# FFN output with eight passing pairs: factors formed in three pieces, bank merges behind later splits, norm scale loaded mid-block

## The chip, the cores and the metric

The kernel runs on one core of one Trainium2 chip. A core has TensorE for matrix products, VectorE (DVE), ScalarE (ACT) and GpSimd (POOL) for elementwise work, SyncE (SP) which here only issues transfers, and 16 DMA engines that all queues share. Each engine works through its own instructions in program order; semaphores tie the engines together. The metric is the device time of one execution in microseconds.

## The reference, cut to what matters

The program is one layer of a decoder: 512 tokens of width 2048, a sparse attention mixer, a SwiGLU feed-forward part, and a final norm. The change touches only the last product of the feed-forward part, and the final norm behind it:

```python
def swiglu(h, w_in, w_out):
    z = h @ w_in
    a, b = z[..., :D_FF], z[..., D_FF:]
    return (jax.nn.silu(a) * b) @ w_out

h = h + swiglu(rmsnorm(h, ffn_norm_g[i]), ffn_w_in[i], ffn_w_out[i])
return rmsnorm(h, final_norm_g)
```

D_FF is 5632, so the last product is (512 x 5632) times (5632 x 2048), in float32.

## The kernel before

**Numbers in two parts.** Float32 accuracy is had from a faster format: each operand is split into a high part (ScalarE copies it into the rounded format) and a low part (VectorE subtracts the high part from the original). A product is three matmuls, high times high, low times high and high times low (`three`, L271 to 274). So each operand costs ScalarE one pass and VectorE one pass before TensorE can use it. Tiles named whi and wlo hold split weights, thi and tlo a split plain factor or split weight sums, ah and al the seven split factors of a pair.

**Units.** The inner dimension is cut into 22 pairs of 256 rows (j), the output columns into four blocks of 512 (b). A unit n is one pair in one block; `ORDER` gives the order of the pairs in each block, `seq` is the list of all 88 units, and the last four (`N_TAIL`) are done together at the end, token tile by token tile. A plain unit is 24 matmuls of 512 columns into the four banks `po`. A unit whose pair is in `SEVEN[b]` uses a Strassen-like scheme: seven products in place of eight, 42 matmuls of 256 columns, into `po` and four more banks `qs` (`seven_unit`). It needs four sums of the weight blocks (`weight_sums`, on VectorE: four 256-column operations, then a split of 768 columns into thi and tlo) and seven factors of the left side (`form`).

**Forms.** `form(j)` loads the pair's left side from DRAM tensor `d_a` into `scratch`, which is the last quarter of the accumulator `acc` before it is needed, makes four sums on VectorE, and splits seven pieces in three steps (256, 512 and 1024 columns; ScalarE L1198, VectorE L894). Five pairs (`KEPT`) stay in SBUF in the pool `asl`. The others are passing pairs: their ah and al go to DRAM (`d_s`, by POOL, L1202) and are loaded again for each later visit (L1222, `load_seven`, POOL) into the two buffers of the pool `ast`. There are nine passing pairs, added block by block: three in block 0, seven in block 1, nine in blocks 2 and 3.

**Order in an iteration.** The program is written in the order in which each engine works; nothing rearranges it. For unit n the loop does: `prepare(n + 1)`, the whole form of the next unit if it is one that forms; `W2.take`, the split of the weights of unit n + 1 (L93 on ScalarE, L95 on VectorE) and the loads of the raw weights behind it (SP, L77, three buffers); `split_a(n + 1)`, the split of a plain unit's left side (L1116), and the load of a later one into one of two homes, `tt` or `rawx` (SP, L1108); the matmuls of unit n; after the block's last seven `merge_sums`, one ScalarE copy and six VectorE additions that bring the four banks `qs` into `acc`; the reloads of passing pairs; and one step of `todo`. After a block, `add` brings `po` into `acc`, and `todo` becomes `ready(b)`, which loads 512 columns of the final norm's scale (`gf`, POOL, L1280) and then, token tile by token tile, sums the squares (ScalarE, L1284) and multiplies by the scale (VectorE, L1285).

**Residual.** What the earlier part left, `d_r`, is loaded into `acc` by POOL: three quarters at the start of this stage (L1226, 3 MB), the last quarter when the last form is done with `scratch` (L1182, 1 MB).

Buffers that matter for waits: whi and wlo four each, thi and tlo two each, `tt` and `rawx` one each, raw three, `ast` two pairs.

Of the kernel before, what the change touches and what calls it, by code (L numbers as in the profile page):

```python
# [10 lines left out]
F32 = mybir.dt.float32  # L11
F32R = mybir.dt.float32r
I32 = mybir.dt.int32
AF = mybir.ActivationFunctionType
# [19 lines left out]
ORDER = [tuple(range(22)),  # L34
# [3 lines left out]
TP_GAP, HN_GAP = 40, 48  # L38
RESYNC = 14
SPREAD = 2560  # L40
# [128 lines left out]
def nsa_block(ctx: ExitStack, tc: tile.TileContext, x, rel_bias, mix_g, ffn_g, fin_g, w_in, w_out,  # L169
              pos_k, w1k, w2k, pos_v, w1v, w2v, f_in, f_out, onehot, out):  # L170
    nc = tc.nc
    mm, act, dve, pool = nc.tensor.matmul, nc.scalar.activation, nc.vector, nc.gpsimd
# [163 lines left out]
    with ExitStack() as st1:  # L336
# [11 lines left out]
        with ExitStack() as st0:  # L348
# [6 lines left out]
            for t in range(NT):  # L355
# [11 lines left out]
            oh = xp.tile([NB + 1, UL + 16 * CL], F32, name="oh")  # L367
# [60 lines left out]
            p = ps1.tile([128, 2, 32], F32, name="tr")  # L428
# [3 lines left out]
            for c0, c1 in ((0, 512), (512, UL), (UL, UL + 496), (UL + 496, UL + 992)):  # L432
                p = ps1.tile([H, 512], F32, name="mlp" if c1 % 1024 == 512 or c1 == UL + 496 else "tr")
# [88 lines left out]
        for i in range(8):  # L522
# [10 lines left out]
            if i == 1:  # L533
                p = ps1.tile([128, 128], F32, name="tr")
# [27 lines left out]
        p = ps1.tile([96, G, 128], F32, name="tr")  # L562
# [8 lines left out]
    with ExitStack() as st2:  # L571
# [206 lines left out]
        for h in range(H):  # L778
# [11 lines left out]
            seq = [(b, kt) for kt in (3, 2, 1, 0) for b in (0, 1)] + [(-1, 0)]  # L790
# [23 lines left out]
    acc = accp.tile([128, NT, D], F32, name="acc")  # L814
# [75 lines left out]
    def f32(t):  # L890
        return t.bitcast(F32)

    def sub(o, a, b):
        dve.tensor_tensor(o, a, b, op=OP.subtract)  # L894

    def plus(o, a, b):
        dve.tensor_tensor(o, a, b, op=OP.add)
# [156 lines left out]
    with tc.tile_pool(name="tmp", bufs=1) as tmp:  # L1054
        todo = sums(tmp)
# [24 lines left out]
        for u in range(2):  # L1080
            k = slice(8 * u, 8 * u + 4)
# [7 lines left out]
    seq = [(b, j) for b in range(4) for j in ORDER[b]]  # L1089
# [20 lines left out]
    def split_a(n):  # L1110
# [36 lines left out]
    for n, (b, j) in enumerate(seq):  # L1147
        if j in SEVEN[b]:
            W2.sums[n] = weight_sums(n)
# [18 lines left out]
    acc = late.tile([128, NT, D], F32, name="acc")  # L1168
    late.tile([128, 16], F32, name="late_gap")
    asl = ctx.enter_context(tc.tile_pool(name="asl", bufs=len(KEPT)))  # L1170
    ast = ctx.enter_context(tc.tile_pool(name="ast", bufs=2))
    late2 = ctx.enter_context(tc.tile_pool(name="late2", bufs=1))
    ss = [late2.tile([128, 4], F32, name=f"sf{t}") for t in range(NT)]
    scratch = acc[:, :, 1536:]
    forms = [n for n, (b, j) in enumerate(seq) if j in SEVEN[b] and (not b or j not in SEVEN[b - 1])]
    visits = [n for n, (b, j) in enumerate(seq) if j in SEVEN[b] and j not in KEPT]

    def load_form(i):
        if i < len(forms):
            nc.sync.dma_start(scratch[:, :2], d_a[seq[forms[i]][1]].rearrange("p (n c) -> p n c", n=2))  # L1180
        else:
            pool.dma_start(scratch, d_r[:, :, 1536:].rearrange("t p c -> p t c"))  # L1182

    def form(j):

        a, m = scratch[:, :2], scratch[:, 2:]
        a11, a21, a12, a22 = a[:, 0, :256], a[:, 0, 256:], a[:, 1, :256], a[:, 1, 256:]
        s1, s3, s2, s4 = m[:, 0, :256], m[:, 0, 256:], m[:, 1, :256], m[:, 1, 256:]
        h, l = ((asl if j in KEPT else ast).tile([128, 1792], F32R, name=f"a{x}") for x in "hl")
        plus(s1, a21, a22)  # L1190
        sub(s3, a11, a21)
        sub(s2, s1, a11)
        sub(s4, a12, s2)
        for c0, c1, src in ((0, 256, a11), (256, 768, a[:, 1]), (768, 1792, m)):
            oh, ol = h[:, c0:c1], l[:, c0:c1]
            if c1 - c0 == 1024:
                oh, ol = (x.rearrange("p (n c) -> p n c", n=2) for x in (oh, ol))
            act(oh, src, AF.Copy)  # L1198
            sub(ol, src, f32(oh))
        if j not in KEPT:  # L1200
            for i, x in enumerate((h, l)):
                pool.dma_start(d_s[j, i], x.bitcast(F32))  # L1202
        keep_seven(j, h, l)
# [8 lines left out]
    n_visit = [0]  # L1212

    def load_seven(n):

# [13 lines left out]
    def prepare(n):  # L1229

        if n in forms:
            form(seq[n][1])
            load_form(forms.index(n) + 1)
            n_visit[0] += n in visits

    def plain_tile(n, w, t, first, last):
        for k in range(2):
# [20 lines left out]
    def merge_sums(b):  # L1258
# [8 lines left out]
        act(u3, qs["p1"], AF.Copy)  # L1267
# [8 lines left out]
    def ready(b):  # L1276

        c = slice(512 * b, 512 * (b + 1))
        gf = late2.tile([128, 512], F32, name="gf")
        pool.dma_start(gf, fin_g[None, c].to_broadcast([128, 512]))  # L1280
        yield
        for t in range(NT):
            junk = late2.tile([128, 1024], F32, name="m")[:, :512]
            act(junk, acc[:, t, c], AF.Square, accum_out=ss[t][:, b:b + 1])  # L1284
            dve.tensor_tensor(acc[:, t, c], acc[:, t, c], gf, op=OP.mult)  # L1285
            yield

    w8, todo = [], iter(())
    n, na = 0, 1
    for b in range(4):  # L1290
        units = ORDER[b][:-N_TAIL] if b == 3 else ORDER[b]
        po = [pf.tile([128, 512], F32, name=f"f{i}") for i in range(4)]
        qs = {x: pf.tile([128, 512], F32, name=f"f{i}") for i, x in enumerate(("p1", "p5", "p6", "p7"))}
        first7 = next(j for j in units if j in SEVEN[b])
        last7 = [j for j in units if j in SEVEN[b]][-1]
        started = False
        for i, j in enumerate(units):
            left = len(units) - 1 - i if b == 3 else 9
            prepare(n + 1)
            w = W2.take(max(1, 3 - left))  # L1300
            while na <= n + 1 + max(0, 2 - left):
                split_a(na)
                na += 1
            if j in SEVEN[b]:
                seven_unit(n, w, first7)
            else:
                for t in range(NT):
                    plain_tile(n, w, t, not started, b < 3 and i == len(units) - 1)
            started = True
            if j == last7:  # L1310
                merge_sums(b)
            load_seven(n)
            if i >= 2:
                next(todo, None)
            n += 1
        if b < 3:
            for t in range(NT):
                add(t, b, po[t])
            todo = ready(b)
    c = slice(1536, 2048)  # L1320
    gf = late2.tile([128, 512], F32, name="gf")
    pool.dma_start(gf, fin_g[None, c].to_broadcast([128, 512]))
    act(warm, epsc, AF.Sqrt)
    for t in range(NT):
        for i in range(N_TAIL):
# [10 lines left out]
        for cb in range(4):  # L1336
            c4 = slice(512 * cb, 512 * (cb + 1))
            src = acc[:, t, c4]
# [33 lines left out]
```

## Time and profile before

| what | value |
|---|---|
| median of 3 runs | 2225.47 us (2224.15 to 2227.64) |
| profiled execution | 2224.97 us |
| its span | 2223.1 us |
| TensorE matmul, busy | 2159.1 us, 97% |
| VectorE, busy | 1573.6 us, 71% |
| ScalarE, busy | 937.9 us, 42% |
| granted clock of TensorE, mean | 0.992 |

The span runs from the first to the last instruction of the profiled execution; what lies between it and that execution's time is start and end of the program. A row of a timeline gives the start from the span's beginning and the duration, both in us, then engine, line, operation, and output and input tiles, and in brackets the idle time before it with what ended it. A row of a group gives busy us and mean ns, and behind the second bar the engine's idle time just before. Matmuls overlap in the pipeline, so a unit is measured from its first matmul's start to the next unit's first start, not by busy time. Where a helper records the operation, all its uses have the same line (L894 is every subtraction of the helper `sub`, L897 every addition of `plus`), so that tiles must be read with it: al<-acc,ah is a form's low part, tlo<-tt,thi of 768 columns the split of weight sums.

### The profile page before, as it was taken

Reading aid. Unit: us, or ns where it says so; the run is one execution under the profiler, and the core shown is the slowest. Engines: PE = TensorE matmul, PEld = TensorE weight load, DVE = VectorE, ACT = ScalarE, POOL = GpSimd, SP = SyncE. Lnnn points to the kernel's source line nnn. Section 1 sums busy time; section 2 is a strip of 40 time slices with the busy share of each in tenths; the row PEclk is TensorE's granted clock in tenths of the full one; section 3 lists DMA queues with packets and bytes.
Section 4 is the critical chain, followed back from the end, with each engine's and each line's share of the span. In section 5 each row is a group of like instructions: output and inputs, shape, how many; then the busy total and the mean of one; then the engine's idle time right before and its main releaser. Section 6 shows DMA issues by size and latency. Waiting matters only on the chain.

```text
span 2223.1 us, 37421 instructions
## 1 busy us (share of the span) xinstructions
PE 2159.1 (97%) x15226; PEld 2004.1 (90%) x15226; DVE 1573.6 (71%) x2587; ACT 937.9 (42%) x1450; POOL 127.2 (6%) x151
## 2 busy tenths in 40 slices
PE   6999999999999999999999999999999999999997
PEld 5889898888989888899999999999999788989886
DVE  5454656656555436898888888888887777877676
ACT  5344444444454224343434443434443444444334
POOL 3100000000012012000000000000000000001010
PEclk9999999999999999999999999999999999999999
DMA  5655323323253542343343334434333776768875
GB/s 166 204 146 156 90 82 96 95 81 95 86 200 110 208 137 101 114 136 122 124 133 122 120 123 131 125 124 133 124 125 117 277 282 227 277 260 300 316 267 184
DMA packets 240588, 350.97 MB, mean 158 GB/s; under 512 B 13055, under 2 KB 178975, under 8 KB 239264
## 3 DMA queue, kind: packets, MB, share of 16 engines
q1 hardware_dynamic: 225040, 266.77, 37.5%
q0 software_dynamic: 14080, 78.67, 9.1%
q10 hardware_dynamic: 1296, 3.15, 0.4%
q8 instruction: 119, 1.95, 0.4%
q14 instruction: 53, 0.43, 0.1%
HBM read 303.61 MB, written 50.17 MB: 159 GB/s over the span
## 4 chain that ended last, share of the span: by engine, by line
PE 83%; DVE 6%; DMA 5%; issue 3%; ACT 2%; POOL 0%; SPq 0%; ACTq 0%; DVEq 0%; POOLq 0%
PE f L273 15%; PE f L274 15%; PE f L272 15%; PE proj L272 8%; PE proj L274 8%; PE proj L273 8%; PE pt L739 2%; DMA tt<-d_a 2%; DVE tlo L894 1%; DMA rawx<-d_a 1%; PE pp L274 1%; PE o L274 1%; PE pp L273 1%; PE pp L272 1%; PE o L273 1%
## 5 line engine op out<-in xcount | busy, mean ns | idle before, releaser
L95 DVE TENSOR_TENSOR wlo<-raw,whi 128x1024 fp32r<-128x1024 f32 (+1 forms) x208 | 252.6, 1217 | 149.2 <-ACT whi L93 148.4
L93 ACT ACTIVATE whi<-raw 128x1024 fp32r<-128x1024 f32 (+1 forms) x226 | 234.4, 1041 | 234.0 <-DVE raw L894 129.5
L894 DVE TENSOR_TENSOR tlo<-tt,thi 128x1536 fp32r<-128x1536 f32 (+2 forms) x136 | 197.3, 1451 | 110.2 <-ACT thi L996 88.2
L272 PE MATMUL f<-hn_h,whi 128*128 128x256 f32 x984 | 271.7, 276 | 0.7 <-ACT E L954 0.7
L273 PE MATMUL f<-hn_l,whi 128*128 128x256 f32 x984 | 271.6, 276 | 0.0
L274 PE MATMUL f<-hn_h,wlo 128*128 128x256 f32 x984 | 271.6, 276 | 0.0
L991 ACT ACTIVATE whi<-raw 128x1024 fp32r<-128x1024 f32 x123 | 126.1, 1057 | 292.5 <-DVE raw L894 282.3
L272 PE MATMUL proj<-hn_h,whi 128*128 128x512 f32 (+1 forms) x544 | 210.2, 386 | 1.0 <-DVE hn_l L261 1.0
L274 PE MATMUL proj<-hn_h,wlo 128*128 128x512 f32 (+1 forms) x544 | 207.5, 381 | 0.0
L273 PE MATMUL proj<-hn_l,whi 128*128 128x512 f32 (+1 forms) x544 | 207.1, 381 | 0.0
L272 PEld LDWEIGHTS f<-hn_h,whi 128*128 128x128 f32 x984 | 184.7, 188 | 1.1 <-ACT E L954 1.1
L274 PEld LDWEIGHTS f<-hn_h,wlo 128*128 128x128 f32 x984 | 184.7, 188 | 0.0
L273 PEld LDWEIGHTS f<-hn_l,whi 128*128 128x128 f32 x984 | 184.7, 188 | 0.0
L996 ACT ACTIVATE thi<-tt 128x1536 fp32r<-128x1536 f32 x82 | 121.8, 1485 | 84.4 <-PE f L273 75.7
L894 DVE TENSOR_TENSOR wlo<-raw,whi 128x1024 fp32r<-128x1024 f32 x123 | 147.0, 1223 | 0.0
L272 PE MATMUL proj<-whi,hn_h 128*128 128x256 f32 (+2 forms) x496 | 146.9, 296 | 0.0
L273 PE MATMUL proj<-wlo,hn_h 128*128 128x256 f32 (+2 forms) x496 | 145.7, 294 | 0.0
L274 PE MATMUL proj<-whi,hn_l 128*128 128x256 f32 (+2 forms) x496 | 145.6, 293 | 0.0
L298 DVE TENSOR_TENSOR ptl<-pt,pth 128x128 fp32r<-128x128 f32 (+3 forms) x128 | 62.6, 489 | 100.5 <-ACT pth L297 100.5
L272 PE MATMUL f<-whi,ah 128*128 128x256 f32 (+1 forms) x416 | 120.6, 290 | 2.0 <-ACT ah L1116 2.0
L274 PEld LDWEIGHTS proj<-hn_h,wlo 128*128 128x128 f32 x544 | 103.9, 191 | 19.8
L274 PE MATMUL f<-whi,al 128*128 128x256 f32 (+1 forms) x416 | 120.5, 290 | 1.1 <-DVE al L894 1.1
(318 smaller groups left out, 6306.3 us busy)
## 6 DMA issues: line engine op xcount, KB each, us to landing
raw<-in_ffn_w_in SPq DMA_DIRECT2D x135, 512.0 KB, 3.6
raw<-in_ffn_w_out SPq DMA_DIRECT2D x88, 512.0 KB, 6.0
raw<-in_nsa_w_in SPq DMA_DIRECT2D x48, 512.0 KB, 3.6
rawx<-in_ffn_w_in SPq DMA_DIRECT2D x41, 512.0 KB, 4.9
ah<-d_s POOLq DMA_DIRECT2D x19, 896.0 KB, 7.5
al<-d_s POOLq DMA_DIRECT2D x19, 896.0 KB, 9.9
raw<-in_nsa_w_out SPq DMA_DIRECT2D x32, 512.0 KB, 3.7
rawx<-d_a SPq DMA_DIRECT2D x32, 512.0 KB, 4.7
```

Of the source, the lines that this page charges most:

```text
L93: self.nc.scalar.activation(hi[:, :n], src, AF.Copy)
L95: eng.tensor_tensor(lo[:, :n], src, hi[:, :n].bitcast(F32), op=OP.subtract)
L272: mm(o, ah, bh, start=start, stop=False, skip_group_check=True)
L273: mm(o, ah, bl, start=False, stop=False, skip_group_check=True)
L274: mm(o, al, bh, start=False, stop=stop, skip_group_check=True)
L298: dve.tensor_tensor(lo, psum_ap, hi.bitcast(F32), op=OP.subtract)
L739: nc.tensor.transpose(pt[rows, 128 * (t - kt):128 * (t - kt + 1)], src, ident)
L894: dve.tensor_tensor(o, a, b, op=OP.subtract)
L991: act(h, r, AF.Copy)
L996: act(h, ttf, AF.Copy)
```

## The change

The change has four parts, all in the FFN output.

1. Other sets and orders. One passing pair fewer: two in block 0, six in block 1, eight in blocks 2 and 3, and other places in the order. 44 units in place of 48 use the seven products, and 13 forms take the place of 14.
2. `form` becomes a generator with three working pieces (sums and two short high parts; two short low parts and the long high part; the long low part, the store to `d_s` and the next load). For a form that unit f needs, the pieces come in the iterations of units f - 4, f - 3 and f - 2, behind the splits for the next unit. Two scratch areas alternate for the forms of blocks 0 and 1, then one; so the residual comes in three loads, 2 MB at the start and 1 MB behind the last early form and the last form each.
3. `merge_sums` is kept pending and done in the next iteration, behind that iteration's splits.
4. The norm scale of a block is loaded on SP in the block's unit 12, in place of POOL at the start of the next block; the steps of `todo` begin at unit 4 of a block instead of unit 2, and one step fewer is there.

```diff
-KEPT = (3, 8, 13, 17, 19)
-SEVEN = [KEPT + x for x in ((5, 10, 15), (5, 10, 15, 0, 1, 2, 4)) + 2 * ((5, 10, 15, 0, 1, 2, 4, 6, 7),)]
+KEPT = (3, 8, 13, 16, 18)
+SEVEN = [KEPT + x for x in ((6, 11), (6, 11, 0, 1, 2, 4)) + 2 * ((6, 11, 0, 1, 2, 4, 5, 7),)]
 ORDER = [tuple(range(22)),
...
+         (3, 5, 6, 7, 0, 9, 8, 10, 1, 12, 11, 13, 14, 2, 16, 15, 17, 4, 18, 19, 20, 21),
+         (6, 9, 3, 11, 10, 5, 8, 12, 0, 13, 14, 1, 15, 7, 16, 2, 17, 18, 4, 19, 20, 21),
+         (6, 9, 3, 11, 10, 0, 8, 1, 12, 2, 13, 4, 14, 5, 16, 7, 18, 15, 17, 19, 20, 21)]
...
-    scratch = acc[:, :, 1536:]
+    scratch = [acc[:, :, 1024:1536], acc[:, :, 1536:]]
...
+    n_early = sum(n < 2 * len(ORDER[0]) for n in forms)
+    form_raw = [scratch[i % 2 if i < n_early else 1] for i in range(len(forms))]
...
+    def load_residual(c):
+        pool.dma_start(acc[:, :, c], d_r[:, :, c].rearrange("t p c -> p t c"))
...
         plus(s1, a21, a22)
         sub(s3, a11, a21)
         sub(s2, s1, a11)
         sub(s4, a12, s2)
...
+        for oh, _, src in parts[:2]:
             act(oh, src, AF.Copy)
+        yield
+        for oh, ol, src in parts[:2]:
             sub(ol, src, f32(oh))
+        act(parts[2][0], m, AF.Copy)
+        yield
+        sub(parts[2][1], m, f32(parts[2][0]))
         if j not in KEPT:
...
+            for k, x in enumerate((h, l)):
+                pool.dma_start(d_s[j, k], x.bitcast(F32))
+        later = [k for k in range(i + 1, len(forms)) if form_raw[k] is form_raw[i]]
+        if later:
+            load_form(later[0])
+        if i + 1 == n_early:
+            load_residual(slice(1024, 1536))
+        if i + 1 == len(forms):
+            load_residual(slice(1536, 2048))
+        yield
...
-    pool.dma_start(acc[:, :, :1536], d_r[:, :, :1536].rearrange("t p c -> p t c"))
+    load_residual(slice(0, 1024))
     load_form(0)
...
+    load_form(1)
+    forming = {n: form(i) for i, n in enumerate(forms)}
...
-            prepare(n + 1)
             w = W2.take(max(1, 3 - left))
             while na <= n + 1 + max(0, 2 - left):
                 split_a(na)
                 na += 1
+            if pending is not None:
+                merge_sums(*pending)
+                pending = None
+            for k in (1, 2, 3, 4):
+                next(forming.get(n + k, iter(())), None)
             if j in SEVEN[b]:
                 seven_unit(n, w, first7)
...
             if j == last7:
-                merge_sums(b)
+                pending = b, qs
             load_seven(n)
-            if i >= 2:
+            if i >= 4:
                 next(todo, None)
+            if i == 12:
+                gf = late2.tile([128, 512], F32, name="gf")
+                nc.sync.dma_start(gf, fin_g[None, 512 * b:512 * (b + 1)].to_broadcast([128, 512]))
```

More of the change, by code (lines that the diff above doesn't have):

```diff
@@ L1173, in nsa_block, with form @@
     ss = [late2.tile([128, 4], F32, name=f"sf{t}") for t in range(NT)]
-    scratch = acc[:, :, 1536:]
+    n_visit = [0]
+    scratch = [acc[:, :, 1024:1536], acc[:, :, 1536:]]
     forms = [n for n, (b, j) in enumerate(seq) if j in SEVEN[b] and (not b or j not in SEVEN[b - 1])]
     visits = [n for n, (b, j) in enumerate(seq) if j in SEVEN[b] and j not in KEPT]
+    n_early = sum(n < 2 * len(ORDER[0]) for n in forms)
+    form_raw = [scratch[i % 2 if i < n_early else 1] for i in range(len(forms))]
+    def load_residual(c):
+        pool.dma_start(acc[:, :, c], d_r[:, :, c].rearrange("t p c -> p t c"))
     def load_form(i):
[L1179 to L1186, printed above, removed]
+        nc.sync.dma_start(form_raw[i][:, :2], d_a[seq[forms[i]][1]].rearrange("p (n c) -> p n c", n=2))
+    def form(i):
+        j = seq[forms[i]][1]
+        a, m = form_raw[i][:, :2], form_raw[i][:, 2:]
         a11, a21, a12, a22 = a[:, 0, :256], a[:, 0, 256:], a[:, 1, :256], a[:, 1, 256:]
@@ L1189, in form @@
         h, l = ((asl if j in KEPT else ast).tile([128, 1792], F32R, name=f"a{x}") for x in "hl")
+        if forms[i] in visits:
+            n_visit[0] += 1
+        keep_seven(j, h, l)
+        parts = [(h[:, :256], l[:, :256], a11), (h[:, 256:768], l[:, 256:768], a[:, 1]),
+                 tuple(x[:, 768:].rearrange("p (n c) -> p n c", n=2) for x in (h, l)) + (m,)]
         plus(s1, a21, a22)
@@ L1193, in form @@
         sub(s4, a12, s2)
[L1194 to L1197, printed above, removed]
+        for oh, _, src in parts[:2]:
             act(oh, src, AF.Copy)
+        yield
+        for oh, ol, src in parts[:2]:
             sub(ol, src, f32(oh))
+        act(parts[2][0], m, AF.Copy)
+        yield
+        sub(parts[2][1], m, f32(parts[2][0]))
         if j not in KEPT:
-            for i, x in enumerate((h, l)):
-                pool.dma_start(d_s[j, i], x.bitcast(F32))
-        keep_seven(j, h, l)
+            for k, x in enumerate((h, l)):
[8 more added lines that the diff above has]
+        yield
     def keep_seven(j, h, l):
@@ L1210, in keep_seven @@
             passing.append(x)
-    n_visit = [0]
     def load_seven(n):
@@ L1224, in load_seven @@
             n_visit[0] += 1
-    pool.dma_start(acc[:, :, :1536], d_r[:, :, :1536].rearrange("t p c -> p t c"))
+    load_residual(slice(0, 1024))
     load_form(0)
[L1229 to L1234, printed above, removed]
+    load_form(1)
+    forming = {n: form(i) for i, n in enumerate(forms)}
     def plain_tile(n, w, t, first, last):
@@ L1256, in seven_unit, with merge_sums @@
                 three(o, lh, ll, *right[name], new, False)
-    def merge_sums(b):
+    def merge_sums(b, qs):
         c = slice(512 * b, 512 * b + 256), slice(512 * b + 256, 512 * b + 512)
@@ L1288, in nsa_block @@
     w8, todo = [], iter(())
-    n, na = 0, 1
+    n, na, pending = 0, 1, None
     for b in range(4):
@@ L1318, in nsa_block @@
                 add(t, b, po[t])
-            todo = ready(b)
+            todo = ready(b, gf)
     c = slice(1536, 2048)
-    gf = late2.tile([128, 512], F32, name="gf")
-    pool.dma_start(gf, fin_g[None, c].to_broadcast([128, 512]))
     act(warm, epsc, AF.Sqrt)
```

5 lines of the change are left out of this document (1 added, 4 removed), and 3 rows, old and new, of the table ORDER.

## The prediction

> **What bounds the kernel now.** I read the page first, then the TensorE timeline at the unit borders of the FFN output, then the groups of VectorE, the waits, and the chain in the stretches where TensorE stood.
>
> ```profile
> span 2223.1 us, 37421 instructions
> PE 2159.1 (97%) x15226; PEld 2004.1 (90%) x15226; DVE 1573.6 (71%) x2587; ACT 937.9 (42%) x1450; POOL 127.2 (6%) x151
> ```
>
> TensorE bounds the whole, so a change can win only what TensorE waits, or matmuls. The stage that the change touches is found by the first matmul of each block of 84 units. The timeline of TensorE, narrowed to these points (start, duration, operation):
>
> ```profile
> 1722.43 0.39 PE L272 MATMUL f<-whi,thi 128*128 128x512 f32 x1
> ...
> 1851.95 0.28 PE L272 MATMUL f<-thi,ah 128*128 128x256 f32 x1
> ...
> 1877.46 0.40 PE L272 MATMUL f<-whi,thi 128*128 128x512 f32 x1
> ...
> 1882.95 0.28 PE L272 MATMUL f<-thi,ah 128*128 128x256 f32 x1
> ...
> 1887.79 0.40 PE L272 MATMUL f<-whi,thi 128*128 128x512 f32 x1
> ...
> 1972.40 0.28 PE L272 MATMUL f<-thi,ah 128*128 128x256 f32 x1
> ...
> 2089.99 0.28 PE L272 MATMUL f<-thi,ah 128*128 128x256 f32 x1
> ...
> 2187.61 0.39 PE L272 MATMUL f<-whi,ah 128*128 128x512 f32 x1
> ```
>
> The rows at 1877.46, 1882.95 and 1887.79 are the starts of a plain unit, a seven-product unit and the next plain one, in an undisturbed place: a plain unit takes 5.49 us, a seven 4.84 us. With these two the blocks of before can be told apart into work and waiting:
>
> - block 0 (8 sevens, 14 plain): 115.6 of 129.5 us, so 13.9 of waiting
> - block 1 (12 and 10): 113.0 of 120.4, 7.5
> - block 2 (14 and 8): 111.7 of 117.6, 5.9
> - block 3 up to the tail (14 and 4): 89.7 of 97.6, 7.9
>
> Together 35.2 us of 465.2. That is all that rearranging can return here. Who makes TensorE wait is VectorE, whose work by shape (the groups of 1722 to 2188; mean ns behind the busy time) is:
>
> ```profile
> L95 DVE TENSOR_TENSOR wlo<-raw,whi 128x1024 fp32r<-128x1024 f32 x86 | 105.0, 1223 | 24.9 <-ACT whi L93 24.9
> L894 DVE TENSOR_TENSOR tlo<-tt,thi 128x768 fp32r<-128x768 f32 x48 | 45.8, 953 | 6.3 <-ACT thi L1139 6.3
> L894 DVE TENSOR_TENSOR tlo<-rawx,thi 128x1024 fp32r<-128x1024 f32 x29 | 35.5, 1223 | 38.6 <-ACT thi L1116 35.6 <-PE f L274 2.8
> ...
> L894 DVE TENSOR_TENSOR tt<-raw 128x256 f32<-128x256 f32 x48 | 20.2, 422 | 8.5 <-DMA raw<-in_ffn_w_out 7.9
> ...
> L894 DVE TENSOR_TENSOR al<-acc,ah 128x1024 fp32r<-128x1024 f32 x14 | 17.2, 1226 | 2.7 <-ACT ah L1198 2.7
> ...
> L894 DVE TENSOR_TENSOR al<-acc,ah 128x512 fp32r<-128x512 f32 x14 | 9.6, 685 | 0.0
> ...
> L897 DVE TENSOR_TENSOR m<-m,f 128x512 f32<-128x512 f32 x8 | 5.5, 686 | 2.5 <-ACT m L1267 2.4
> ...
> L897 DVE TENSOR_TENSOR m<-m,f 128x1024 f32<-128x1024 f32 x4 | 4.9, 1221 | 0.4
> ```
> ```profile
> L1139 ACT ACTIVATE thi<-tt 128x768 fp32r<-128x768 f32 x48 | 40.1, 835 | 10.9 <-PE f L274 6.7 <-PE f L273 2.6 <-DVE wlo L95 1.3
> ```
>
> Preparing a seven costs VectorE 4 x 0.42 + 1.22 + 0.95 = 3.9 us, a plain unit 2 x 1.22 = 2.4, one form 5 x 0.42 + 0.69 + 1.23 = 4.0, one bank merge 4 x 0.69 + 2 x 1.22 = 5.2. Since thi and tlo have two buffers, tlo of a unit can start only when the unit before the running one is over; of the 4.84 to 5.49 us until it is needed, thi on ScalarE (0.84) and tlo itself (0.95 or 1.22) take about 2. So VectorE may carry about 2.7 us of other work in between before TensorE stands. A form of 4.0 is over that, and before it stands ahead of the splits of its own unit. Here is one on VectorE:
>
> ```profile
> 1762.58 1.23 DVE L894 TENSOR_TENSOR tlo<-tt,thi 128x1024 fp32r<-128x1024 f32 x1 [5.50 <-ACT thi L1116]
> ...
> 1766.40 1.23 DVE L894 TENSOR_TENSOR al<-acc,ah 128x1024 fp32r<-128x1024 f32 x1 [0.19 <-ACT ah L1198]
> ...
> 1770.69 0.95 DVE L894 TENSOR_TENSOR tlo<-tt,thi 128x768 fp32r<-128x768 f32 x1
> ```
>
> After tlo of unit 7 (late by a transfer, 5.50 idle) VectorE forms until 1767.6, and tlo of unit 8 ends at 1771.6, while a unit of 5.49 is running.
>
> **The change, part by part.**
>
> *Four sevens fewer* (44 for 48: KEPT and the passing pairs 6, 11, 0, 1, 2, 4, 5, 7): 44 x 4.84 + 40 x 5.49 = 432.6 against 48 x 4.84 + 36 x 5.49 = 430.0. Cost +2.6 us on TensorE, on the path, with nothing that hides it.
>
> *Forms in pieces, behind the splits.* 13 for 14. The pieces are 4 x 0.42 = 1.7, then 0.42 + 0.69 = 1.1, then 1.23, one per unit, each under the 2.7. Where two forms overlap it is at most 1.7 + 1.23 = 2.9 in one unit. Block 0 after has 7 sevens, 15 plain units, 7 forms and one merge: 27 + 37 + 28 + 5 = 97 us of VectorE, about 100 with four bank adds of the 512 shape (0.69), in 116 of TensorE; so the work fits, and what was wrong before was its lumps. Each first piece takes a buffer of the passing pairs, whose reader two visits earlier must be over; by the order it is, by one unit at the tightest (first piece in unit 31, 45, 53; reader in 30, 44, 52), and ScalarE stands there behind a thi that waits for the same unit. SP gets load_form behind the third piece; it waits for VectorE there, as the raw loads behind it do anyway. Block 0's 13.9: unit 1's start-up of about 1 us stays, I leave 1.5 more. Saved 11.4.
>
> *The bursts of transfers.* Blocks 1 and 2 lose where a form's store, a reload and (once) the residual go out together. The chain, the windows and the transfers of the stage (KB each, median us to landing):
>
> ```profile
> 1731.60 11.81 DMA rawx<-d_a
> ...
> 1950.14 13.54 DMA tt<-d_a
> ...
> 2047.22 12.01 DMA ah<-d_s
> ```
> ```profile
> 2045.25:2069.57 24.32, 20.99 (x147) 19.82 (x145) 16.89 (x30) 8.24 (x9) 3.92 (x7) 0.93 0.94 356
> 1940.99:1965.00 24.01, 20.09 (x130) 17.73 (x129) 17.03 (x23) 8.33 (x9) 3.70 (x7) 1.00 0.97 377
> ```
> ```profile
> raw<-in_ffn_w_out SPq DMA_DIRECT2D x84, 512.0 KB, 6.3
> ah<-d_s POOLq DMA_DIRECT2D x19, 896.0 KB, 7.5
> ...
> d_s<-ah POOLq DMA_DIRECT2D x9, 896.0 KB, 6.7
> ...
> acc<-d_r POOLq DMA_DIRECT2D x1, 3072.0 KB, 15.2
> ...
> acc<-d_r POOLq DMA_DIRECT2D x1, 1024.0 KB, 9.9
> ```
>
> The last three figures of a window row are granted clock, DMA share and GB/s: in both stretches the transfers are the limit (0.94 and 0.97). After, the ah half of a store goes out a unit ahead of its al half, and stores come two units ahead of the form's use, so at the end of block 1 I count from unit 36 to 42 a store 1.84 MB, the second residual 1.05, a reload 1.84, six raws 3.1 and three plain loads 1.6: 9.4 MB in about 27 us, 350 GB/s, just under the 377 that the row shows. At the end of block 2 the pattern store, last residual, reload, reload stays; but a raw is asked for when the VectorE split three units back is done, and that is 4 us earlier without a form ahead of it. At the start 2 MB of residual go instead of 3. Three reloads and one store fewer (16 for 19, 8 for 9). I leave 1.5 us in each of blocks 1 and 2: saved 6.0 and 4.4. Bounds: nothing left, and all of the 13.4 that these two blocks lose.
>
> *The norm scale.* POOL, then VectorE, in block 3, and the wait:
>
> ```profile
> 2106.32 0.54 POOL L1280 DMA_DIRECT2D gf<-in_final_norm_g  x1
> ```
> ```profile
> 2106.06 0.96 DVE L894 TENSOR_TENSOR tlo<-tt,thi 128x768 fp32r<-128x768 f32 x1 [0.17 <-ACT thi L1139]
> 2116.27 0.69 DVE L1285 TENSOR_TENSOR acc<-acc,gf 128x512 f32<-128x512 f32 x1 [9.25 <-DMA gf<-in_final_norm_g]
> ...
> 2120.02 0.95 DVE L894 TENSOR_TENSOR tlo<-tt,thi 128x768 fp32r<-128x768 f32 x1
> ```
> ```profile
> POOL ah L1222 <- PE f L274: 129.2, 13, 17.2
> ...
> DVE acc L1285 <- DMA gf<-in_final_norm_g: 9.3, 1, 9.3
> ```
>
> On POOL the load stands behind reloads that wait for TensorE (17.2 us the longest), and VectorE, first in its queue, stands 9.25 us for it with the splits of unit 71 behind it. After, it is issued on SP in unit 12 of the block before, some 14 units ahead of its use, with its buffer free since unit 7. Block 3's 7.9 goes to 0.5: saved 7.4. If SP were late, 14 units of cover would have to go first.
>
> *Merges one iteration later.* 5.2 us of VectorE move behind the next unit's splits; three plain units follow the last seven in blocks 0 to 2 (16.5 us of TensorE against 3 x 2.4 + 5.2 + the next seven's 3.9 = 16.3), so nothing is gained or lost beside the block sums. In block 3 the merge leaves its place ahead of the tail's al and falls ahead of the last wlo: I take 0, with 0.7 either way, by the size of one plain term (1.23) less its cover.
>
> *A leftover wait costs more than itself:*
>
> ```profile
> 1753.52:1756.93 3.41, 3.21 (x15) 3.21 (x16) 3.41 (x4) 1.80 (x2) 0.00 (x0) 0.50 0.99 396
> 1835.44:1838.85 3.41, 3.41 (x19) 3.41 (x18) 1.63 (x3) 0.90 (x2) 0.00 (x0) 0.50 0.92 297
> ```
>
> TensorE is busy nearly throughout both stretches, yet at a granted clock of 0.50: 1.7 us lost in each, which the block sums hold already. The Trainium skill, TensorE: Matmul & The Clock Gate, section Part 1: The HAM clock gate, says that half speed comes after an idle window of about 3.4 us; by that rule leftover waits of 1 to 2 us keep full speed and the sum stands, while if two of them drop the clock as in these rows the time is 3.4 higher, 2201.8.
>
> **Sum.** Saved 11.4 + 6.0 + 4.4 + 7.4 = 29.2, less 2.6: 26.6 us. The profiled execution took 2224.97 with a span of 2223.1; 2224.97 - 26.6 = 2198.4. The median of the runs shown, 2225.47, is 0.5 above the profiled one, so I do not shift the sum.
>
> **Rivals.**
>
> - *The bursts stay.* For it: 0.94 and 0.97 in the two windows, and the same bytes per unit after. Then blocks 1 and 2 keep 11.5 instead of 3.0 and block 0 one more: 9.5 less, 2207.9. The Trainium skill, DMA: Bandwidth & Descriptors, section Specifications, gives a core about 358 GB/s of HBM; by it my 350 would be at the limit and this rival likelier, but the row with 377 GB/s is above that figure, and the measurement decides.
> - *VectorE stays the bound in block 0.* Moving a form to other units does not shrink it; with splits that follow close, two overlapping forms (2.9) exceed the 2.7. Against it: 100 of 116 us. If 10 of the 11.4 stay: 2208.4.
> - *Slower: ScalarE is caught by an early form.* Piece one writes a passing buffer. Should ScalarE be a whole unit ahead there, it waits for that buffer's reader with the next whi behind it, up to 4.84 us at each of the six passing forms of blocks 1 and 2: 29.0, so 2227.4. It turns the sign from 4.4 us per form on. Against it: the thi ahead of it waits for the same unit.
> - *All waits but start-up go:* residue 1.1 instead of 6.0, 2193.5.
>
> **How the numbers follow.** Forecast (6 us of residue, 2195 to 2204) 0.47; all waits gone 0.15; bursts stay 0.18; VectorE bound 0.10; both of these, with most of 35.2 kept, 2221 and so no change, 0.03; ScalarE caught 0.07. A difference under 0.2% (4.5 us) is about what a measurement of this kernel cannot tell from none. Faster 0.90, same 0.03, slower 0.07. The range 2191 to 2211 takes in the first four cases with the clock's 3.4 on either of them.
>
> **What would show it.** Right: unit starts a plain 5.49 or seven 4.84 apart through block 0; no wait of VectorE on gf; no half-clock stretch near the old unit 71; TensorE in the stage near 433 plus 6. Wrong: chain entries of ten us and more for rawx, tt or raw near the ends of blocks 1 and 2; ScalarE's ah waiting for TensorE; VectorE waiting for a raw after the 1 MB residuals.

## The result, and the profile after

The changed kernel takes 2194.49 us (median of 4 runs, 2191.91 to 2195.54) against 2226.55 for the kernel before beside it: ratio 0.985, 95% interval 0.983 to 0.987. The prediction said 2198.4 with a range of 2191 to 2211. Faster was right, and the time lies in the range, but nearer to the rival without waits (2193.5). The profiled execution took 2191.91 us.

The page after, and TensorE's timeline at the first matmul of each block and of the tail (start, duration, operation):

```profile
span 2190.2 us, 37229 instructions
PE 2146.6 (98%) x15154; PEld 1993.1 (91%) x15154; DVE 1564.2 (71%) x2564; ACT 935.7 (43%) x1447; POOL 121.4 (6%) x140
```
```profile
1720.32 0.39 PE L272 MATMUL f<-whi,thi 128*128 128x512 f32 x1
...
1837.33 0.28 PE L272 MATMUL f<-thi,ah 128*128 128x256 f32 x1
...
1950.83 0.28 PE L272 MATMUL f<-thi,ah 128*128 128x256 f32 x1
...
2063.19 0.28 PE L272 MATMUL f<-thi,ah 128*128 128x256 f32 x1
...
2152.89 0.39 PE L272 MATMUL f<-whi,ah 128*128 128x512 f32 x1
```

With 4.84 us for a seven and 5.49 for a plain unit, block 0 (7 sevens, 15 plain) is 116.2 us of work in 117.0, block 1 (11, 11) 113.6 in 113.5, block 2 (13, 9) 112.3 in 112.4, block 3 up to the tail (13, 5) 90.4 in 89.7. A remainder below zero is sevens that follow a seven, which take 4.77, and some plain units of 5.44. So the 35.2 us of waiting are gone but for the start-up of unit 1 (1.1) and 0.58 in unit 59, and the stage up to the tail takes 432.57 us for 465.17.

Between the two profiled executions the span falls by 32.9: 32.6 in the stage, 2.1 ahead of it, where nothing was changed, less 1.75 in the tail (37.28 for 35.53). The part ahead of the stage ended between 1718.67 and 1725.66 us in the profiles of this case, so kernels that ran once are compared below by the stage and the tail, not by their time.

The transfers at the ends of blocks 1 and 2 are as dense as before. The last three figures of a window row are granted clock, DMA share and GB/s:

```profile
1910.00:1934.00 24.00, 24.00 (x165) 22.10 (x164) 16.65 (x21) 10.36 (x11) 3.50 (x7) 1.00 1.01 382
2020.00:2045.00 25.00, 24.63 (x192) 23.48 (x191) 15.07 (x20) 10.12 (x11) 2.10 (x4) 1.00 0.99 382
```

The share is 1.01 and 0.99, above the 0.97 and 0.94 of before, and yet TensorE (the first busy figure) is busy for all of the first window and all but 0.4 us of the second. Full DMA engines alone did not make TensorE wait. The chain still names one transfer of over ten us, a reload near the end of block 2, and only unit 59's 0.58 us of waiting stand behind it:

```profile
2012.39 14.67 DMA al<-d_s
```

The tail got longer, by 1.75 us. VectorE and TensorE there, and two windows of 3.4 us, the second of them at half clock:

```profile
2152.56 1.23 DVE L894 TENSOR_TENSOR al<-tt,ah 128x1024 fp32r<-128x1024 f32 x1
2153.70 0.68 DVE L897 TENSOR_TENSOR m<-m,f 128x512 f32<-128x512 f32 x1
...
2157.72 1.22 DVE L897 TENSOR_TENSOR acc<-acc,m 128x1024 f32<-128x1024 f32 x1
2158.86 1.22 DVE L95 TENSOR_TENSOR wlo<-raw,whi 128x1024 fp32r<-128x1024 f32 x1
2160.00 1.22 DVE L894 TENSOR_TENSOR al<-rawx,ah 128x1024 fp32r<-128x1024 f32 x1
```
```profile
2160.14 0.49 PE L273 MATMUL f<-wlo,ah 128*128 128x512 f32 x1 [2.57 <-DVE wlo L95]
2161.27 0.50 PE L274 MATMUL f<-whi,al 128*128 128x512 f32 x1 [0.64 <-DVE al L894]
```
```profile
2158.42:2161.83 3.41, 1.05 (x3) 0.67 (x4) 2.79 (x3) 0.00 (x0) 0.00 (x0) 1.00 0.00 0
...
2161.80:2165.20 3.40, 3.40 (x9) 2.63 (x8) 1.45 (x4) 0.72 (x2) 0.00 (x0) 0.50 0.00 0
```

The last merge (2153.70 to 2158.94) stands ahead of wlo and al of the last unit. TensorE waits 2.57 and 0.64 us for them, and the next 3.4 us run at clock 0.50, 1.7 us lost.

### The profile page after: what moved, and what is told of

The parts are those of the page before. It is cut to its first block, busy times and chain, and to the rows that moved or that the text cites. A ratio compares the mean times of both kernels' runs of the same rounds, so it can differ in the third digit from the quotient of the medians.

```text
span 2190.2 us, 37229 instructions
## 1 busy us (share of the span) xinstructions
PE 2146.6 (98%) x15154; PEld 1993.1 (91%) x15154; DVE 1564.2 (71%) x2564; ACT 935.7 (43%) x1447; POOL 121.4 (6%) x140
## 4 chain that ended last, share of the span: by engine, by line
PE 93%; DVE 3%; DMA 2%; ACT 1%; issue 1%; SPq 0%; POOL 0%; ACTq 0%; DVEq 0%; POOLq 0%
PE f L274 18%; PE f L273 18%; PE f L272 18%; PE proj L272 8%; PE proj L274 8%; PE proj L273 8%; PE pt L739 2%; PE pp L274 1%; PE pp L272 1%; PE pp L273 1%; PE o L274 1%; PE o L273 1%; PE s L272 1%; PE s L274 1%; PE o L272 1%; PE s L273 1%
## 5 line engine op out<-in xcount | busy, mean ns | idle before, releaser
L274 PE MATMUL f<-whi,tlo 128*128 128x512 f32 x320 | 125.0, 391 | 0.7 <-DVE tlo L894 0.6
L273 PE MATMUL f<-wlo,thi 128*128 128x512 f32 x320 | 125.0, 391 | 0.0
L272 PE MATMUL f<-whi,thi 128*128 128x512 f32 x320 | 124.7, 390 | 0.0
```

What stands on the lines that cost most here:

```text
L272: mm(o, ah, bh, start=start, stop=False, skip_group_check=True)
L273: mm(o, ah, bl, start=False, stop=False, skip_group_check=True)
L274: mm(o, al, bh, start=False, stop=stop, skip_group_check=True)
```

## The experiments

Twelve kernels, by the same reading. Waits are each block's length less 4.84 and 5.49 per unit. Stage, waits and tail are those of one profiled execution; so is the time, but for the two marked *, where it is the median of 4 runs.

| kernel | time | stage to tail | waits, blocks 0 / 1 / 2 / 3 | tail |
|---|---|---|---|---|
| before | 2224.97 | 465.17 | 13.9 / 7.5 / 5.9 / 7.9 | 35.53 |
| changed | 2191.91 | 432.57 | 0.8 / -0.1 / 0.0 / -0.7 | 37.28 |
| e1: before, new sets and order | 2208.9 | 449.36 | 6.6 / 6.2 / 4.7 / -0.7 | 37.17 |
| e10: changed, old sets and order | 2210.1 | 446.61 | 1.5 / 8.3 / 4.7 / 2.1 | 36.84 |
| e7: before, scale loaded mid-block | 2214.0 | 452.63 | 11.6 / 7.3 / 4.1 / -0.3 | 35.06 |
| e4: changed, scale loaded as before | 2196.8 | 435.20 | 1.7 / 1.2 / 0.4 / -0.7 | 37.59 |
| e2: changed, whole late forms | 2211.1 | 446.57 | 2.0 / 8.7 / 4.0 / -0.7 | 38.32 |
| e3: changed, whole early forms | 2200.9 | 440.05 | 1.5 / 7.3 / -0.6 / -0.7 | 37.17 |
| e11: e2, residual loads later | 2207.0 | 440.27 | 2.0 / 6.6 / -0.2 / -0.7 | 39.30 |
| e13: e10, residual loads later | 2201.6 | 441.18 | 1.6 / 4.7 / 2.8 / 2.1 | 37.60 |
| e6: changed, merges at once | 2197.2 | 432.95 | 1.4 / -0.4 / 0.1 / -0.7 | 37.65 |
| e9: changed, last merge at once | 2197.4 | 435.11 | 2.9 / -0.4 / 0.8 / -0.7 | 37.10 |
| e8*: changed, last merge late | 2193.15 | 432.79 | 1.9 / -0.4 / -0.6 / -0.7 | 36.05 |
| e12*: changed, last merge in two | 2190.95 | 433.55 | 1.3 / -0.4 / 0.8 / -0.7 | 33.60 |

e8, e9 and e12 differ from the changed kernel in nothing ahead of the end of block 3, and yet their stages spread from 432.57 (the changed kernel's) to 435.11 us, their block 0 waits from 0.8 to 2.9, block 2 from -0.6 to 0.8, block 1 only from -0.4 to -0.1. A difference of that size between two rows is read below as none.

**e1, the sets and the order alone.** The kernel before, with the new KEPT, SEVEN and ORDER:

```diff
-KEPT = (3, 8, 13, 17, 19)
+KEPT = (3, 8, 13, 16, 18)
...
```

> The kernel before with the new sets and orders of pairs alone (44 sevens, 13 forms); forms whole, merges at once, norm scale on POOL as before. Theory (lumps: VectorE's queue holds a whole form, and once the norm scale's wait, ahead of the splits that TensorE needs): the lumps stay, so of the 35.2 us of waiting in the 84 units some 25 to 33 stay and 2.6 us of matmuls come on top: about the time of the kernel before, 2215 to 2228 us. Rival (bursts of transfers set the waits, and the new order alone spreads them): the waits of blocks 1 and 2 (13.4 us) mostly go, 2208 to 2214 us.

18.4 of the 35.2 us of waiting go with the sets and the order alone: 7.3 in block 0 and all of block 3, though the scale of the norm is still loaded on POOL at the block's start. The time lies in the rival's range, but not for its reason: blocks 1 and 2 keep 10.9 of their 13.4. POOL in block 3, with the new order:

```profile
2085.50 0.53 POOL L1222 DMA_DIRECT2D ah<-d_s  x1 [20.14 <-PE f L274]
2086.02 0.53 POOL L1222 DMA_DIRECT2D al<-d_s  x1
2086.54 0.54 POOL L1280 DMA_DIRECT2D gf<-in_final_norm_g  x1
```

One reload stands ahead of the scale after the block's start at 2080.31. Before, two did, each waiting for a unit:

```profile
2095.18 0.53 POOL L1222 DMA_DIRECT2D ah<-d_s  x1 [14.70 <-PE f L274]
2095.70 0.53 POOL L1222 DMA_DIRECT2D al<-d_s  x1
2105.28 0.53 POOL L1222 DMA_DIRECT2D ah<-d_s  x1 [9.04 <-PE f L274]
2105.79 0.53 POOL L1222 DMA_DIRECT2D al<-d_s  x1
2106.32 0.54 POOL L1280 DMA_DIRECT2D gf<-in_final_norm_g  x1
```

So the new order issues the load 6.2 us into the block in place of 16.3 (2106.32 less 2089.99), early enough.

**e7, the norm scale alone, in the kernel before.**

```diff
+            if i == 12:
+                gf = late2.tile([128, 512], F32, name="gf")
+                nc.sync.dma_start(gf, fin_g[None, 512 * b:512 * (b + 1)].to_broadcast([128, 512]))
...
-            if i >= 2:
+            if i >= 4:
                 next(todo, None)
```

> The kernel before, with nothing changed but the load of the norm scale: on SP in unit 12 of the block, steps of the norm from unit 4. Theory of the prediction (the load costs 7.4 us of block 3): 2218 to 2220, block 3 under 1 us of waiting. Rival (behind VectorE's wait for the scale stands another late transfer, and the new order with one passing pair fewer is what removed it): under 3 us, 2222.5 to 2226.5, block 3 keeps 5 or more.

Block 3 goes from 7.9 to -0.3 and blocks 0 and 2 lose 2.3 and 1.8 as well: 12.5 us off the stage, and a time below both ranges. In the order of before, the late scale did cost what block 3 waited. That the other blocks gain was not foreseen, and is not shown to come from the load: it is about what kernels with the same code there differ by, and block 0 of before has no load of the scale at all.

**e4, the norm scale put back on POOL at the start of the next block, in the changed kernel.**

```diff
-            if i == 12:
-                gf = late2.tile([128, 512], F32, name="gf")
-                nc.sync.dma_start(gf, fin_g[None, 512 * b:512 * (b + 1)].to_broadcast([128, 512]))
...
+        gf = late2.tile([128, 512], F32, name="gf")
+        pool.dma_start(gf, fin_g[None, c].to_broadcast([128, 512]))
+        yield
```

> The changed kernel with the norm scale loaded by POOL at the start of the next block's steps, as before. Lumps: VectorE waits for the scale in block 3, where POOL's reloads wait for TensorE; 5 to 9 us of TensorE's waiting return there, with a stretch at half clock: 2197 to 2203 us. Rival (with the new order POOL is free in time, or the load was a matter of the burst alone): under 2 us, 2192 to 2196 us.

Here the stage is 2.6 us longer, about as e9's is (2.5) with the same code up to the end of block 3, and block 3 waits for nothing. Only the 1.3 us of block 1 (units 27 and 28) are more than that spread. The order and the new place of the load each cure block 3, so the second to come finds little left.

**e10, all of the change but the sets and the order:** nine passing pairs and 48 sevens in the changed kernel, with KEPT, SEVEN and ORDER of before.

```diff
-KEPT = (3, 8, 13, 16, 18)
+KEPT = (3, 8, 13, 17, 19)
...
```

> The changed kernel with the sets and the order of before: nine passing pairs, 48 units of seven products. Theory 'the early pieces suffice': 2.6 us less of matmuls, no waits but start-up, 2190 to 2193. Rival 'the eighth pair less is needed' (the sets alone took away 18 of 35 us of waits, and four more units with a reload or store keep the transfers too dense): blocks 1 and 2 or block 3 wait 4 to 12 us again, 2196 to 2204.

16.6 us of waits stay, more than either theory had, against 16.8 in e1. Neither half does without the other: the code takes away block 0's waits, and only both together take away those of blocks 1 and 2. Four sevens given up cost 2.6 us and return 16.6.

**e2, forms whole and ahead of their own unit's splits**, the rest as changed:

```diff
+            for _ in forming.get(n + 1, ()):
+                pass
             w = W2.take(max(1, 3 - left))
...
-            for k in (1, 2, 3, 4):
-                next(forming.get(n + k, iter(())), None)
```

> The changed kernel with each form done whole, ahead of the splits of its own unit, one unit ahead, as before; sets, merges and norm scale as changed. Lumps: waits return in block 0, 8 to 12 us there (7 forms), 1 to 2 us for each of the other six forms, together 12 to 22 us, so 2205 to 2215 us. Rival (bursts): block 0 stays within 3 us of its 117.0, since its transfers are the same, and the sum rises by less than 6 us, mostly at the ends of blocks 1 and 2.

Block 0 waits 2.0 and not 8 to 12: with the new sets, whole forms ahead of the splits cost it next to nothing. The waits return at the ends of blocks 1 and 2, and the chain there names transfers (start, us, what):

```profile
1935.40 14.59 DMA tt<-d_a
...
2029.76 13.82 DMA al<-d_s
```

In the changed kernel the same load of tt, of the groups of DMA issues between 1925 and 1935 us (KB each, median us to landing), takes half as long:

```profile
tt<-d_a SPq DMA_DIRECT2D x1, 512.0 KB, 7.5
```

**e11, e2 with the two late residual loads moved:**

```diff
-        if i + 1 == n_early:
-            load_residual(slice(1024, 1536))
-        if i + 1 == len(forms):
-            load_residual(slice(1536, 2048))
...
+            if n == 51:
+                load_residual(slice(1024, 1536))
+            if n == 67:
+                load_residual(slice(1536, 2048))
```

> The kernel with whole forms ahead of their own unit's splits (2211.1 us, waits of 7.7 us in units 41 and 42 and 4.0 in unit 59), where only the two late 1 MB loads of the residual are moved: from behind the forms of units 39 and 57 to units 51 and 67. VectorE's and ScalarE's instructions stay as they are. Theory 'bursts': 1.05 MB at 377 GB/s are 2.8 us less in each of the two places, so their 11.7 us fall to 6 or less, 2203 to 2206. Rival 'lumps' (VectorE's whole form ahead of the splits is what makes TensorE wait): 10 us or more stay, 2209 to 2212.

No instruction of VectorE or ScalarE differs, yet block 2's waits go from 4.0 to -0.2: there the burst is the cause, shown. In block 1 only 2.1 of 8.7 go; unit 41 loses 2.10 us for 4.83, unit 42 still 2.47. The load of tt still took 12 us there:

```profile
1936.91 12.14 DMA tt<-d_a
```

So 6.3 of the 12.7 us are the residual's collision with the store and the reloads of the same place.

**e3, forms whole but early, behind the splits of iteration f - 3:**

```diff
-            for k in (1, 2, 3, 4):
-                next(forming.get(n + k, iter(())), None)
+            for _ in forming.get(n + 3, ()):
+                pass
```

> The changed kernel, but each form is made whole, behind the splits, in the iteration of unit f - 3: early, but not in pieces. Theory 'early' (what helps is that the store, the residual and the next load of a form leave two units earlier, and that the form stands behind the splits): waits of the four blocks stay under 3 us together, 2194 to 2199. Rival 'pieces' (4.0 us of a whole form are over the 2.7 us that VectorE has spare in a unit): about 1.3 us for each of 13 forms, 10 to 17 us, spread over blocks 0 to 2 with block 0 at 5 or more, 2204 to 2212.

Neither theory holds whole. Blocks 0 and 2 need no pieces: a form of 4.0 us in one unit costs nothing there. Block 1 loses 7.3, in units 30 and 31 (3.36 and 2.34) and 43 (1.92). The chain ahead of unit 30's end:

```profile
1869.34 1.07 ACT ah L1209
1870.43 0.64 DVE al L894
...
1872.18 1.22 DVE wlo L95
1873.40 1.14 DVE tlo L894
1874.56 13.30 DMA rawx<-d_a
1887.94 1.07 ACT thi L1116
```

The form stands ahead of the tlo that sets rawx free, so the load is asked for at 1874.56; and the form's store and the reload behind it, 3.67 MB in all, were put out on POOL just ahead of it:

```profile
1870.69 0.53 POOL L1214 DMA_DIRECT2D d_s<-ah  x1 [19.35 <-ACT ah L1209]
1871.95 0.53 POOL L1214 DMA_DIRECT2D d_s<-al  x1 [0.73 <-DVE al L894]
1872.48 0.54 POOL L1239 DMA_DIRECT2D ah<-d_s  x1
1873.01 0.54 POOL L1239 DMA_DIRECT2D al<-d_s  x1
```

In the changed kernel SP asks for the same rawx 2.3 us into unit 28 in place of 4.0, and the store's halves leave 5.8 us apart, with the load between them:

```profile
1870.65 0.34 SPq L1108 DMA_DIRECT2D rawx<-d_a  x1
```
```profile
1866.27 0.54 POOL L1214 DMA_DIRECT2D d_s<-ah  x1 [2.02 <-ACT ah L1209]
1872.05 0.54 POOL L1214 DMA_DIRECT2D d_s<-al  x1 [5.24 <-DVE al L894]
```

What a lump on VectorE costs here is not its 4 us but the later request behind its own burst. The load still takes 11.0 us in the changed kernel, but it lands 13.4 us after the start of unit 28 in place of 17.3, and TensorE does not wait for it. That each of the two, the request and the spreading of the store, does its part was not separated.

**e13, e10 with the residual loads moved** (to units 53 and 67, as in e11):

> The changed kernel with nine passing pairs in the order of before (2210.1 us, waits of 8.3, 4.7 and 2.1 us in blocks 1 to 3), where only the two late 1 MB loads of the residual are moved to units 53 and 67. Theory 'density of transfers': 2.8 us less in each place, waits of units 42 to 44 (9.5 us) and of 61 to 67 (5.2) fall by half or more, 2201 to 2205. Rival 'the reloads themselves' (one per two units in block 3 and the pair at units 38 and 40 are too dense, whatever the residual does): 12 us of waits or more stay, 2206.5 to 2212.

16.6 us of waits become 11.2, the stage is 5.4 shorter. Units 42 and 61 are cured; 43 and 44 (3.55 and 2.97) and 66 and 67 (1.57 and 1.33) are not. A third of these waits was the residual's place; with nine pairs the rest stays, and its cause was not tried further.

**e6 and e9, merges at once**, in all blocks (the diff) and in the last alone:

```diff
             if j == last7:
-                pending = b, qs
+                merge_sums(b, qs)
```

> The changed kernel with all four merges at once, in the iteration of the block's last seven-product unit, as in the kernel before. Theory of the prediction (the later merge neither gains nor loses in blocks 0 to 2; at once in block 3 leaves the tail at 37.1 us): waits of blocks 0 to 2 as in the changed kernel within 1 us each, 2192 to 2198. Rival (5.2 us of VectorE ahead of the next splits, where the load that a split sets free is then asked for late, as with a whole form): 2 to 4 us of waiting behind the last seven-product unit of blocks 0, 1 and 2 (units 19, 41 and 63), 2199 to 2207.

> The changed kernel with the last block's merge alone at once, in unit 82's iteration as in the kernel before, not one iteration later. Theory 'the delay of the merge costs the tail 1.75 us': tail back to 35.0 to 35.8, no half-clock stretch in the first 15 us of the tail, 2190 to 2193.5. Rival (the merge then stands ahead of the splits of units 85 to 87 together, and the waits are as long, only earlier): tail 36.5 to 38, or 1 us and more of waiting in unit 83.

In e6 the waits of blocks 0 to 2 differ from the changed kernel's by 0.6 at most: the later merge gains and loses nothing there, as predicted. In the tail it doesn't help to go back: 37.65 and 37.10, and e1, with the old code and its merge at once, has 37.17. At once, the merge stands ahead of the splits of units 85 to 87 together, and e9's TensorE waits about as long in smaller parts:

```profile
2161.39 0.50 PE L274 MATMUL f<-whi,al 128*128 128x512 f32 x1 [0.81 <-DVE al L894]
2165.88 0.50 PE L272 MATMUL f<-whi,ah 128*128 128x512 f32 x1 [1.93 <-ACT ah L1116]
```

A half-clock stretch follows at 2166.4. The kernel before has waits of this size in its tail too, but no such stretch after them (the last section has the reason); from its first matmul to the next tile's, the first token tile takes 9.35 us before, 9.80 after, 10.41 in e9.

**e8 and e12, the last merge later.** e8 puts all of it behind the splits of the last unit; e12 puts only its two long additions there:

```diff
 def merge_sums(b, qs):
         ...
         plus(acc[:, 2:, c[0]], acc[:, 2:, c[0]], halves(u3))
+        yield
         mm2 = m.rearrange("p (a c) -> p a c", a=2)
...
-                merge_sums(*pending)
+                rest = merge_sums(*pending)
+                next(rest)
+                if b < 3:
+                    next(rest, None)
...
+        next(rest, None)
         add(t, 3, po[t])
```

> The changed kernel with the last block's merge put behind all splits of the last four units, ahead of the first bank add. In the changed kernel the 5.2 us of that merge stand ahead of wlo and al of the last unit, and TensorE waits 2.8 + 0.9 us there, with 3.4 us at half clock behind. Theory: the wait falls to under 1 us, the tail from 37.3 to about 33 us, so 4 us less, near 2190 us. Rival (the tail waits for the transfer of the last plain factor, and the first token tile's bank add then waits for the merge): tail 36 to 37.3 us, under 1.3 us of gain.

> The changed kernel with the last block's merge cut in two: its copy and four short additions stay where they are, the two long additions come behind the splits of the last unit (wlo and al of unit 87), ahead of the first bank addition of the tail. Theory 'the merge is ahead of the last splits' (2.8 and 0.9 us of waiting in the tail, and a 3.4 us stretch at half clock behind them that costs 1.7): the splits come 2.4 us earlier, the first token tile ends about 7.1 us after the tail's start instead of 9.4, the long additions delay VectorE by about 1 us there, which it makes up at 0.3 us per tile; tail 33.7 to 35.5 instead of 37.3, median 2190.5 to 2193. Rival (as when the whole merge went behind the splits, VectorE's own chain per tile becomes the bound): tail 36 or more, median 2193 to 2195.

e8 shortens the first token tile to 6.86 us, but its bank addition then waits behind the merge (2158.34 to 2163.58 on VectorE), and VectorE needs about 5.1 us for a tile's chain where TensorE needs 5.44, so the delay lives on: tail 36.05. In e12 the splits fall between the merge's parts:

```profile
2155.34 0.69 DVE L897 TENSOR_TENSOR acc<-acc,m 128x512 f32<-128x512 f32 x1
2155.95 1.22 DVE L95 TENSOR_TENSOR wlo<-raw,whi 128x1024 fp32r<-128x1024 f32 x1
2157.09 1.22 DVE L894 TENSOR_TENSOR al<-rawx,ah 128x1024 fp32r<-128x1024 f32 x1
2158.22 1.21 DVE L897 TENSOR_TENSOR m<-m,f 128x1024 f32<-128x1024 f32 x1
...
2160.80 0.69 DVE L821 TENSOR_TENSOR acc<-acc,f 128x512 f32<-128x512 f32 x1
```

The second tile starts 7.17 us after the first, no half-clock stretch lies ahead of the last matmul, and the tail is 33.60, 3.7 less than in the changed kernel. Over 4 runs e12 takes 2190.95 us (2187.52 to 2193.45), ratio to before 0.985, interval 0.983 to 0.987; e8 2193.15, ratio 0.986, 0.983 to 0.988. By these intervals neither is told apart from the changed kernel; the shorter tail is seen in one profiled execution each.

## Why the prediction was right, and where not

- **Four sevens fewer, +2.6.** Right: the stage is 432.57 us, and the prediction's count of work alone 432.6.
- **The leftover of 6.0 us.** This term failed, by nearly all of its size: 1.1 us of unit 1's start-up and 0.6 in unit 59 are left, and sevens that follow a seven give as much back. It is the whole of the miss in the stage: the sum had 26.6 of gain, the stage gave 32.6. The 6.0 was an allowance, not read from a row.
- **Block 0, 11.4 by pieces behind the splits.** The saving came, the reason fell, so the size was right by luck. Whole forms ahead of the splits wait 2.0 us in block 0 (e2) and whole early ones 1.5 (e3); with the old code and the new sets it is 6.6 (e1), so about 7 us went with the sets and the order. Of the code, the 2 MB of residual at the start in place of 3 and the second scratch area are left as causes. The traces point at the residual: the load of rawx that is asked for 3.71 us into unit 1 took 11.81 us before and 11.89 in e1, each behind 3 MB, and 9.28 in e2 behind 2 MB; the load of tt in unit 2 took 9.31 in e1, where the chain names it, and 5.96 in e2. No run changes the residual's size alone. The prediction's own row of 11.81 us for rawx lies in block 0 and named a transfer; the prediction charged the block to VectorE. The bound of 2.7 us that VectorE may carry in a unit does not hold: the nine forms of blocks 0 and 2 in e3, 4.0 us each in one unit, went with 0.6 us of waiting (unit 2) beside the start-up.
- **Blocks 1 and 2, the bursts.** The saving came, 13.4 for 10.4. That bursts made the waits is shown, with whole forms, for block 2 and a quarter of block 1 (e11). That bytes per time decide is wrong: the windows after are fuller (382 GB/s, share 1.01 and 0.99) and nothing waits. Earlier requests and stores that are earlier and spread do it, together: e2 against the changed kernel is 12.8 us in these two blocks. The rival that bursts stay took the density for the cost and fell. The Trainium skill, DMA: Bandwidth & Descriptors, section Specifications, gives about 358 GB/s of HBM per core; the trace does not agree, with 382 held for 24 us.
- **The norm scale, 7.4.** The price was right where it was read (e7: 8.2 in block 3), but in this change the order alone pays it (e1). A load that was late by its place in a queue was cured twice, and the sum came out right because the prediction counted it once.
- **Merges, 0 with 0.7 either way.** Right in blocks 0 to 2 (e6). In block 3 the tail lost 1.75, more than the bound. The step that failed is "less its cover": what was counted was VectorE's time; what came was a half-clock stretch of 1.7 us behind waits that are no longer than before's in all (about 4.0 us for 3.9). That the later merge brought it is not shown: e1, e6 and e9, with the merge at once, have such a stretch in the tail too.
- **The rivals.** VectorE as the bound in block 0 and ScalarE caught by an early form did not come: with 0.8, -0.1, 0.0 and -0.7 us of waiting the block sums leave no room for either.

## What to carry over

Where loads are asked for by the engine that frees their buffer, cost a long step on that engine by what it does to the request: a 4 us step that also puts out 3.7 MB just ahead of a 0.5 MB load made that load take 13.3 us and made TensorE wait, while the same load, asked for 1.7 us earlier in its unit between the parts of the store, took 11.0 and hid in full. Before moving a late load, look at what stands ahead of it in its queue; here the order of other work already cured it. And in a tail that goes tile by tile, put long additions between the last splits and the first tile's end, not ahead of the splits: that tail is 33.60 us for 37.28, in one profiled execution.

## What was not expected of the hardware

Half-clock stretches follow waits that are far from filling 3.4 us. Ahead of the stretch at 2161.8 of the changed kernel TensorE was busy 1.05 us of 3.41; ahead of the one at 1753.52 before, 1.43:

```profile
1750.11:1753.52 3.41, 1.43 (x6) 0.74 (x4) 3.04 (x5) 2.94 (x4) 0.37 (x1) 1.00 0.99 333
```

In 26 such stretches, all that the fourteen kernels have between the start of the stage and the last matmul, the waits in the 3.41 us ahead, summed from the matmuls' starts, were 2.1 to 3.4 us; e12, with 1.6 us in its tail, has none. Two waits of 1.30 and 1.28 us close together in e7 (from 1833.25) had none either. Where they lie decides. The stretches of one kernel begin on one grid of 3.413 us: those of before, at 1753.52, 1835.44, 1965.14, 2064.13 and 2118.74, are 24, 38, 29 and 16 such steps apart. Along each kernel's grid the stage and the tail make 1879 windows at full clock; the 26 with 2.13 us of waits or more are each followed by half clock, and none of the others, with 2.08 or less, is. The pair in e7 falls on two windows, with 1.55 and 1.14.

This is also why the tail of before has no stretch. Its waits fall on three windows, with 0.80, 1.34 and 1.74 us, those of the changed kernel on two, with 1.22 and 2.73. The last two windows of before:

```profile
2190.42:2193.84 3.42, 2.26 (x10) 1.50 (x8) 1.91 (x2) 0.28 (x1) 0.00 (x0) 1.00 0.47 153
2193.84:2197.25 3.41, 2.06 (x8) 1.41 (x9) 1.32 (x2) 0.77 (x1) 0.00 (x0) 1.00 0.02 5
```

Its longest wait there, 2.14 us with 0.69 shortly behind it, would fit into one window. The grid lies elsewhere against the span's start in each profile, so whether a tail with such waits pays the 1.7 us is luck.

The Trainium skill, TensorE: Matmul & The Clock Gate, section Part 1: The HAM clock gate, speaks of free-running windows of 3413 ns and of half speed after an idle one; the trace agrees with the length (stretches of 3.4 and 6.8 us) and with windows that start where they like, not with a window that has to be idle throughout.
